# Dealing out two side generators more tightly: HGRN's steps earlier, some gate steps last

## The chip, the cores and the metric

The kernel runs on one core of a Trainium2 chip. The metric is the device time of one execution in microseconds (us); before the change the median of three runs was 3617.13 us (3607.03 to 3620.99). A profiled execution took 3613.31 us.

## The reference

Two networks run one after the other on 512 tokens of width 1024. The change is in the first block, which mixes three branches:

```python
xn = rmsnorm(x, norm1_w[l])
p = xn @ w_in[l]
z, xbc, dt_raw, p_rwkv, p_hgrn, p_gate = jnp.split(p, in_splits, axis=-1)
y_ssm = ssd_branch(z, xbc, dt_raw, ...) @ w_branch_ssm[l]
y_rwkv = rwkv7_branch(p_rwkv, ...) @ w_branch_rwkv[l]
y_hgrn = hgrn2_branch(p_hgrn, ...) @ w_branch_hgrn[l]
gates = jax.nn.sigmoid(p_gate).reshape(b, L, N_BRANCH, D_MODEL)
mixed = gates[:, :, 0] * y_ssm + gates[:, :, 1] * y_rwkv + gates[:, :, 2] * y_hgrn
x = x + mixed @ w_out[l]
```

The RWKV branch is a delta-rule recurrence in two directions for 8 heads of 64; the HGRN branch is a gated linear recurrence in two directions for 4 heads of 128; the gates are 24 blocks of 128 columns of the projection. The second block (attention, a neighbourhood attention, an mLSTM and a differential attention, twice) is not touched.

## The kernel before

Every projection is held in float16 halves: a block of 128 x 128 weights takes three matmuls (high x high, high x low, low x high) of 512 columns each. Weights come in units of 8 blocks (512 KB). `_emit_unit` loads a unit with a DMA on SP's queue, ScalarE writes the high half (L1070) and VectorE the low half (L1071). There are two buffer pairs for the foreground (`whi`, `wlo`) and two for the background (`bhi`, `blo`). Units are prefetched in the order of two written lists, FOREGROUND and BACKGROUND; `take` checks that the code uses them in just that order, and a unit's pair comes free when its last matmul has read it.

The first phase (`first`, pool `f_rwkv`) runs RWKV in four stages of two heads. A stage j is `rwkv_mid` (products with the decays, matrices G, a loop of 31 rows in which VectorE solves triangular blocks at L464 and L467, with DMAs before and behind it to turn the data round) and then `rwkv_scan` (8 chunks, each a chain TensorE to VectorE and back; its first VectorE instruction is L526), and at the end `rwkv_out`. Inside the scan of stage j, at chunk 2, `rwkv_in` makes the inputs of stage j + 1: it takes three weight units and uses the PSUM bank `acc`; at chunk 4 come their decays.

Two Python generators are dealt out between those steps by `beside(g, h)`. It adds g to what is due of the gates and h to what is due of HGRN, and advances each by its whole steps. A gate step is one weight block, three matmuls into the bank `bg1`, with 8 steps in a gate block and 192 in all; the gates use the foreground's list. HGRN has 15 steps a head and 60 in all: 5 of projections, 7 levels, 2 states, 1 output; its weights are of the background's list and its projections use `bg0`. `beside` is called 7 times in `rwkv_mid` (each fourth row) and 8 times in `rwkv_scan`. What is left behind the last stage is traced by `beside(1000, 1000)`. Then the pool closes and SSD begins (`ssd`, its first instruction is `dsk` at L617), with the three up-projections as background behind it.

The order in which this is traced is a priority, not the order on the engines: a scheduling pass goes through the program with a model of times and gives each engine, whenever it is free, the earliest traced instruction that is ready. The order that it finds is then fixed, and each engine executes its own in order. So a traced step may be drawn ahead of its place where its buffers, banks and weights allow it. A tile of a new pool waits until the tiles that lay there before are done.

Of the kernel before, what the change touches and what calls it, by code (L numbers as in the profile page):

```python
# [226 lines left out]
def run(gen):  # L227

    try:
        while True:  # L230
            next(gen)
    except StopIteration as e:
        return e.value

class First:
# [39 lines left out]
    def rwkv(self, yd, beside):  # L275


        nc, v = self.nc, self.nc.vector
        mid = self.mid
        it = self.block_iter("w1", 0, 14)  # L280
        self.mu2 = self.t(mid, [128, 14], "mu2")
        v.tensor_tensor(out=self.mu2, in0=self.col("mu0", 0, 14), in1=self.col("mu1", 0, 14), op=ALU.add)
        v.tensor_scalar(out=self.mu2, in0=self.mu2, scalar1=-1.0, scalar2=1.0, op0=ALU.mult, op1=ALU.add)
        self.hb = self.t(mid, [128, 12], "hb1")
        v.tensor_scalar(out=self.hb, in0=self.col("wa0", 0, 12), scalar1=0.5, scalar2=None, op0=ALU.mult)
        self.ka1 = self.t(mid, [128, 4], "ka1")
        v.tensor_scalar(out=self.ka1, in0=self.col("ka", 0, 4), scalar1=-1.0, scalar2=1.0, op0=ALU.mult, op1=ALU.add)
        self.lwh, self.lwl = (self.t(mid, [128, 3, T], n, F16) for n in ("lwh", "lwl"))
        for n in range(3):
            lw = self.w()  # L290
            nc.sync.dma_start(out=lw, in_=self.io["lora"][:, n])
            self.split(self.lwh[:, n], self.lwl[:, n], lw, WS)
        lx, gx = (tuple(self.t(mid, [128, T], n + p, F16) for p in "hl") for n in ("lx", "gx"))
        c = self.w()
        run(self.shifted(it, 12, c))
        nc.scalar.activation(out=c[0:64], in_=c[0:64], func=AF.Tanh)
        self.split(*lx, c)
        c = self.w()
        run(self.shifted(it, 13, c))
        nc.scalar.activation(out=c, in_=c, func=AF.Tanh, scale=0.5)  # L300
        v.tensor_scalar(out=c, in0=c, scalar1=0.5, scalar2=0.5, op0=ALU.mult, op1=ALU.add)
        self.split(*gx, c)
        self.hsel = self.load(mid, "hsel", [128, 2])
        self.hexp = self.load(mid, "hexp", [2, 128])
        self.hones = self.load(mid, "hones", [128, 128])
        self.rwm = self.load(mid, "rwm", [128, 2, 128])
        self.reset = self.t(mid, [128, T + 64], "reset")
        v.memset(self.reset, 1.0)
        v.memset(self.reset[:, 0::64], 0.0)  # L309
        run(self.rwkv_in(0, it, lx))  # L310
        self.rwkv_decays(0, lx)
        for j in range(4):
            self.rwkv_mid(j, beside)
            scan = self.rwkv_scan(j)
            for c in range(8):
                if c == 2 and j < 3:
                    run(self.rwkv_in(j + 1, it, lx))
                if c == 4 and j < 3:
                    self.rwkv_decays(j + 1, lx)
                next(scan)  # L320
                beside(2.5, 1)
            run(scan)
            self.rwkv_out(j, gx, yd)

# [72 lines left out]
    def rwkv_mid(self, j, beside):  # L397
# [61 lines left out]
        for i in range(31):  # L459
            ts, nt = slice(i + 1, 32), 31 - i  # L460
            rs = [(c, (i - 2 * c) // 4 + 1) for c in range(2) if i >= 2 * c]
            for c, n in rs:
                t = tx[c][:, 0:n * nt].rearrange("p (a b) -> p a b", b=nt)
                v.tensor_tensor(out=t, in0=X[c][:, 0:n, i:i + 1].to_broadcast([128, n, nt]), in1=M[:, i:i + 1, ts].to_broadcast([128, n, nt]), op=ALU.mult)  # L464
            for c, n in rs:
                t = tx[c][:, 0:n * nt].rearrange("p (a b) -> p a b", b=nt)
                v.tensor_tensor(out=X[c][:, 0:n, ts], in0=X[c][:, 0:n, ts], in1=t, op=ALU.subtract)  # L467
            if i % 4 == 3:
                beside(3.5, 0.9)
        pd2 = self.t(self.dram, [2, 32, 8, 2, 2, 32], "pd2")  # L470
        for q in range(2):
            for c in range(2):
# [491 lines left out]
class Net(First):  # L964
# [1160 lines left out]


FOREGROUND = [
# [35 lines left out]
```

## Time and profile before

| | |
|---|---|
| median of three runs | 3617.13 us |
| profiled execution | 3613.31 us |
| its span, first to last instruction | 3611.6 us |
| instructions | 60781 |
| TensorE busy | 3338.2 us (92%) |
| VectorE busy | 2760.1 us (76%) |
| ScalarE busy | 1608.3 us (45%) |
| GpSimd busy | 752.6 us (21%) |
| granted TensorE clock, mean | 0.976 |

Busy time counts from an instruction's start to its end. Matmuls overlap, so a busy TensorE is not one at its peak: the distance between two starts tells how many go in a microsecond. Times in the rows count from the span's start. The first phase lies in the first fifth of the span.

### The profile page before, as it was taken

To read this page: it belongs to the slowest core of one execution; us is meant where nothing else is said; L and a number is where in the kernel's file an instruction comes from. 1 tells how busy PE (TensorE), PEld (TensorE's weight loads), DVE (VectorE), ACT (ScalarE), POOL (GpSimd) and SP (SyncE) were. 2 spreads that over 40 slices of the span, in tenths; PEclk is the share of its full clock that TensorE was granted. 3 is DMA by queue.
4 is the path that set the end of the run, shared out by engine and by line. 5 is a ranking of instruction groups with operands and counts; after the bars stand their busy time and mean duration, and the time that the engine had idled before them with its cause. 6 is when DMAs were issued, how large, how long until landed. Compare 5 with 4: busy or idle time off the path is not lost. (4 is left out here: it accounts for less than half of the span.)

```text
span 3611.6 us, 60781 instructions
## 1 busy us (share of the span) xinstructions
PE 3338.2 (92%) x23758; PEld 2033.9 (56%) x23758; DVE 2760.1 (76%) x5599; ACT 1608.3 (45%) x3009; POOL 752.6 (21%) x782
## 2 busy tenths in 40 slices
PE   7899999899899999999989999999999989999998
PEld 3565566555455577556545545568655545545567
DVE  6877777587777798788767677788788767777788
ACT  4232333255344344464556543344364455534443
POOL 2222223223332211201221132211201120132211
PEclk9999999899899999999999999999999999999999
DMA  4312213233242234323223353335322323363333
GB/s 141 82 57 59 75 49 91 72 126 114 88 164 94 94 106 146 106 63 96 93 82 109 116 159 96 96 112 159 111 65 80 94 90 100 112 185 110 94 100 94
DMA packets 151156, 368.16 MB, mean 102 GB/s; under 512 B 44098, under 2 KB 47428, under 8 KB 150868
## 3 DMA queue, kind: packets, MB, share of 16 engines
q1 hardware_dynamic: 117492, 336.03, 30.0%
q0 software_dynamic: 7680, 23.00, 1.9%
q10 hardware_dynamic: 25696, 5.25, 0.8%
q8 instruction: 186, 3.05, 0.4%
q14 instruction: 102, 0.84, 0.1%
HBM read 322.72 MB, written 40.04 MB: 100 GB/s over the span
## 5 line engine op out<-in xcount | busy, mean ns | idle before, releaser
L1181 PE MATMUL acc<-xh,whi 128*128 128x512 f16 x1224 | 469.5, 384 | 28.3 <-DVE g L1706 7.5
L1183 PE MATMUL acc<-xh,wlo 128*128 128x512 f16 x1224 | 469.0, 383 | 23.7 <-DVE wlo L1071 23.6
L1182 PE MATMUL acc<-xl,whi 128*128 128x512 f16 x1224 | 468.9, 383 | 0.0
L1070 ACT ACTIVATE whi<-wst 128x1024 f16<-128x1024 f32 x264 | 275.3, 1049 | 310.3 <-PE acc L1182 147.1
L1071 DVE SCALAR_TENSOR_TENSOR wlo<-wst,whi 128x1024 f16<-128x1024 f32 x264 | 353.9, 1341 | 15.9 <-ACT whi L1070 14.3
L1183 PEld LDWEIGHTS <-wlo 128*128 128x128 f16 x1824 | 179.6, 98 | 257.3 <-DVE wlo L1071 51.4
L1182 PEld LDWEIGHTS <-whi 128*128 128x128 f16 x1824 | 179.9, 99 | 226.6 <-issue 41.9
L1181 PEld LDWEIGHTS <-whi 128*128 128x128 f16 x1824 | 180.6, 99 | 210.4 <-issue 12.4
L1183 PE MATMUL bg<-xh,blo 128*128 128x512 f16 x596 | 230.9, 387 | 3.4 <-DVE reset L309 3.2
L1181 PE MATMUL bg<-xh,bhi 128*128 128x512 f16 x596 | 230.9, 387 | 0.4 <-DVE hk L810 0.4
L1182 PE MATMUL bg<-xl,bhi 128*128 128x512 f16 x596 | 230.6, 387 | 0.0
L1440 POOL TENSOR_TENSOR w<-w,w 128x512 f32<-128x512 f32 x66 | 117.5, 1780 | 448.4 <-DVE w L1440 282.1
L1216 PE MATMUL acc<-whi,xh 128*128 128x128 f16 x1152 | 195.1, 219 | 3.1 <-DVE xp L1758 1.3
L1218 PE MATMUL acc<-whi,xl 128*128 128x128 f16 x1152 | 195.0, 219 | 0.0
L1217 PE MATMUL acc<-wlo,xh 128*128 128x128 f16 x1152 | 195.0, 219 | 0.0
L1070 ACT ACTIVATE bhi<-bst 128x1024 f16<-128x1024 f32 (+1 forms) x132 | 121.7, 934 | 129.4 <-PE bg L1182 89.7
L1071 DVE SCALAR_TENSOR_TENSOR blo<-bst,bhi 128x1024 f16<-128x1024 f32 (+1 forms) x132 | 160.8, 1223 | 13.7 <-ACT bhi L1070 12.1
L1183 PE MATMUL bg<-xh,wlo 128*128 128x512 f16 x408 | 157.3, 386 | 9.1 <-DVE wlo L1071 9.1
L1181 PE MATMUL bg<-xh,whi 128*128 128x512 f16 x408 | 157.4, 386 | 3.0 <-ACT whi L1070 1.8
L1182 PEld LDWEIGHTS <-bhi 128*128 128x128 f16 x980 | 97.6, 100 | 109.0 <-issue 20.1
L1183 PEld LDWEIGHTS <-blo 128*128 128x128 f16 x980 | 97.5, 100 | 106.9 <-issue 6.8
L1181 PEld LDWEIGHTS <-bhi 128*128 128x128 f16 x980 | 97.9, 100 | 105.4 <-issue 9.8
(666 smaller groups left out, 9256.9 us busy)
## 6 DMA issues: line engine op xcount, KB each, us to landing
wst<-win SPq DMA_DIRECT2D x92, 512.0 KB, 3.6
bst<-win SPq DMA_DIRECT2D x64, 512.0 KB, 3.7
wst<-wff SPq DMA_DIRECT2D x60, 512.0 KB, 3.5
wst<-w SPq DMA_DIRECT2D x58, 512.0 KB, 3.6
gd<-bw SPq DMA_DIRECT2D x88, 256.0 KB, 2.2
ug<-gd SPq DMA_DIRECT2D x88, 256.0 KB, 2.7
wst<-wf SPq DMA_DIRECT2D x30, 512.0 KB, 3.5
bst<-w SPq DMA_DIRECT2D x20, 512.0 KB, 3.6
```

Source lines behind the costliest of these rows:

```text
L1070: nc.scalar.activation(out=hi[:, h], in_=st[:, h], func=AF.Copy, scale=WS)
L1071: nc.vector.scalar_tensor_tensor(out=lo[:, h], in0=st[:, h], scalar=WS, in1=hi[:, h], op0=ALU.mult, op1=ALU.subtract)
L1181: mm(ps, lhsT=wh, rhs=h[:, k, :], start=(k == 0), stop=False)
L1182: mm(ps, lhsT=wh, rhs=l[:, k, :], start=False, stop=False)
L1183: mm(ps, lhsT=wl, rhs=h[:, k, :], start=False, stop=(k == nk - 1))
L1216: mm(o, lhsT=xh, rhs=wh, start=(k == 0), stop=False)
L1217: mm(o, lhsT=xh, rhs=wl, start=False, stop=False)
L1218: mm(o, lhsT=xl, rhs=wh, start=False, stop=(k == 7))
L1440: tt = lambda eng, o, x, y, op=ALU.add: eng.tensor_tensor(out=o, in0=x, in1=y, op=op)
```

## The change

In the scan each chunk deals out 2 gate steps and 1.25 HGRN steps, where it was 2.5 and 1; in the mid part each fourth row deals out 3 and 1.1, where it was 3.5 and 0.9. The foreground's weight list follows the new order of use: between RWKV's second and third group of units stand four gate units instead of six, and behind the last group eleven instead of nine.

```diff
                 next(scan)
-                beside(2.5, 1)
+                beside(2, 1.25)
             run(scan)
...
             if i % 4 == 3:
-                beside(3.5, 0.9)
+                beside(3, 1.1)
...
 FOREGROUND = [
-    ("w1", 0, 5), ("w1", 14, 18), ("w1", 5, 8), ("w1", 18, 24), ("w1", 8, 11), ("w1", 24, 29),
-    ("w1", 11, 14), ("w1", 29, 58), ("wo1", 0, 8), ("wf1", 0, 2), ("wf1s", 0, 1), ("wf1", 2, 6),
+    ("w1", 0, 5), ("w1", 14, 18), ("w1", 5, 8), ("w1", 18, 22), ("w1", 8, 11), ("w1", 22, 27),
+    ("w1", 11, 14), ("w1", 27, 58), ("wo1", 0, 8), ("wf1", 0, 2), ("wf1s", 0, 1), ("wf1", 2, 6),
```

Units 0 to 13 of `w1` are RWKV's (the first two for the low-rank inputs, then three a stage), 14 to 37 the gates', 38 to 57 SSD's.

## Rows read from the trace of the kernel before

**Rows 1.** Busy time by stretch: RWKV's four stages, and behind them.

```profile
core 0: us, PE busy (x) PEld busy (x) DVE busy (x) ACT busy (x) POOL busy (x), PEclk, DMA share, GB/s
97.90:235.90 138.00, 126.74 (x1046) 84.26 (x1045) 107.72 (x276) 42.17 (x91) 36.18 (x36) 0.98 0.24 66
235.90:398.30 162.40, 150.40 (x1133) 97.42 (x1132) 122.62 (x308) 49.83 (x103) 45.80 (x43) 0.94 0.22 64
398.30:544.30 146.00, 138.33 (x1094) 90.68 (x1093) 113.25 (x297) 47.49 (x93) 40.60 (x36) 0.98 0.23 66
544.30:677.50 133.20, 124.49 (x1037) 85.82 (x1037) 95.19 (x271) 43.80 (x92) 42.09 (x29) 0.97 0.25 75
677.50:712.00 34.50, 20.33 (x165) 13.57 (x164) 15.96 (x61) 4.05 (x15) 7.32 (x10) 0.61 0.34 117
```

**Rows 2.** Timeline, VectorE, L526 in stage 1's scan: start us, us, engine, line.

```profile
308.23 0.42 DVE L526 TENSOR_SCALAR w<-O 64x256 f32<-64x256 f32 x1
...
321.47 0.42 DVE L526 TENSOR_SCALAR w<-O 64x256 f32<-64x256 f32 x1 [0.48 <-PE O L524]
...
347.88 0.41 DVE L526 TENSOR_SCALAR w<-O 64x256 f32<-64x256 f32 x1
...
367.31 0.41 DVE L526 TENSOR_SCALAR w<-O 64x256 f32<-64x256 f32 x1
```

**Rows 3.** Groups, TensorE, 128 to 174 us: xcount | busy us, mean ns | idle before.

```profile
L1183 PE MATMUL acc<-xh,wlo 128*128 128x512 f16 x24 | 10.1, 422 | 1.9 <-DVE wlo L1071 1.9
```

**Rows 4.** Groups, TensorE, 300 to 345 us.

```profile
L1183 PE MATMUL acc<-xh,wlo 128*128 128x512 f16 x24 | 9.4, 391 | 0.0
```

**Rows 5.** Timeline, ScalarE, splits of weights in stage 1's scan.

```profile
327.73 1.06 ACT L1070 ACTIVATE whi<-wst 128x1024 f16<-128x1024 f32 x1 [1.89 <-PE acc L1182]
...
343.43 1.06 ACT L1070 ACTIVATE whi<-wst 128x1024 f16<-128x1024 f32 x1 [7.81 <-PE acc L1182]
```

**Rows 6.** Timeline, VectorE, L526 in stage 3's scan: first, seventh and eighth.

```profile
616.19 0.42 DVE L526 TENSOR_SCALAR w<-O 64x256 f32<-64x256 f32 x1
...
666.43 0.42 DVE L526 TENSOR_SCALAR w<-O 64x256 f32<-64x256 f32 x1 [1.86 <-PE O L524]
...
672.61 0.42 DVE L526 TENSOR_SCALAR w<-O 64x256 f32<-64x256 f32 x1 [1.77 <-PE O L524]
```

**Rows 7.** Timeline, all engines, the end of the phase and SSD's start.

```profile
686.42 1.27 POOL L586 TENSOR_TENSOR w<-w,bon 128x512 f32<-128x512 f32 x1 [3.37 <-DVE w L585]
...
694.50 0.69 DVE L917 TENSOR_TENSOR hw<-hw,hg 128x512 f32<-128x512 f32 x1
...
696.46 0.17 DVE L617 TENSOR_SCALAR dsk<-cols 128x8 f32<-128x8 f32 x1 [1.27 <-PE H L1547]
...
701.43 0.42 ACT L1231 ACTIVATE wdh<-wdt 128x256 f16<-128x256 f32 x1 [4.17 <-DMA wdt<-wdt]
```

**Rows 8.** Timeline, TensorE, two matmuls of a row.

```profile
155.36 0.38 PE L1183 MATMUL acc<-xh,wlo 128*128 128x512 f16 x1
155.57 0.38 PE L1181 MATMUL acc<-xh,whi 128*128 128x512 f16 x1
```

**Rows 9.** Groups, TensorE, 25 to 700 us, HGRN's largest.

```profile
L1181 PE MATMUL bg<-xh,bhi 128*128 128x512 f16 x95 | 38.4, 404 | 0.4 <-DVE hk L810 0.4
...
L1216 PE MATMUL bg<-bhi,xh 128*128 128x128 f16 x256 | 49.8, 235 | 13.2 <-DVE hi L816 9.9 <-DVE hk L810 3.3
...
L852 PE MATMUL H<-hw,hw 128*128 128x128 f32 x160 | 25.2, 291 | 9.6 <-DVE tx L464 6.0 <-DVE hs L832 2.4 <-DVE hw L847 1.3
```

**Rows 10.** Groups, VectorE, 25 to 700 us: weight splits, HGRN's level operations.

```profile
L1071 DVE SCALAR_TENSOR_TENSOR wlo<-wst,whi 128x1024 f16<-128x1024 f32 x38 | 53.2, 1399 | 3.0 <-ACT whi L1070 2.0 <-PE bg L1183 0.9
...
L867 DVE TENSOR_TENSOR hp<-hp 128x512 f32<-128x512 f32 x28 | 24.7, 882 | 0.4
...
L846 DVE TENSOR_TENSOR hw<-hq,hp 128x512 f32<-128x512 f32 x28 | 22.4, 799 | 0.1
```

**Rows 11.** One line's instructions, L867: ns min/median/max, first and last start.

```profile
L867 DVE TENSOR_TENSOR hp<-hp x28: 673/692/1751, 136.0 to 658.9; 128x512 f32<-128x512 f32 x28
```

## The prediction

> **What bounds the kernel now.** I read the page's line of 40 slices first: in the first phase TensorE is at 7 to 9 tenths and VectorE at 7 to 8, so neither is simply full. Then the busy time by stretch, cut at the start of each RWKV stage [rows 1]. The reader is to see three things in it. The four stages have nearly the same work and take 138.0, 162.4, 146.0 and 133.2 us (the last has no inputs of a next stage to make). In all four TensorE is busy for 92 to 95% and VectorE for 71 to 78%. And behind the last stage lies a gap, 677.5 to 712 us, in which TensorE is busy for 20.3 of 34.5 us at a granted clock of 0.61, which is between its two levels of 1.2 and 2.4 GHz, and VectorE for 16.0 us.
>
> Then I read the steps of the RWKV scan in the timeline of VectorE, by their first instruction there, L526. In stage 1 most follow each other in about 7 us, but from 321.47 to 367.31 us two take 45.84 us together; the two before them took 13.24 [rows 2]. What lies there? By the groups of TensorE, the three weight units of RWKV's next inputs (24 matmuls of each of three lines, into the bank acc) run at 300 to 345 us, inside that scan [rows 4]; in stage 0 the same work ran at 128 to 174 us, inside the mid part, ahead of the scan, which starts at 172 [rows 3]. ScalarE's splits of those units in stage 1 both wait for the last matmul of the unit before (releaser PE acc L1182), 15.7 us apart [rows 5]: the other pair of weight buffers is held by a gate unit. So the order of the weight list, not any engine, puts this work into the scan: in stage 0 four gate units stand between RWKV's third-last and next units, in stage 1 six.
>
> Last, the end. HGRN's last head closes after RWKV: RWKV's last read of its own pool is GpSimd's L586, 686.42 + 1.27 = 687.69 us; HGRN's last product ends at 695.19, and SSD's first instruction, dsk, starts at 696.46, waiting for the transposes of it [rows 7]. The pool of the first phase must be empty before SSD's tiles are written.
>
> **The change part by part.** Per stage there are 7 calls in the mid part and 8 in the scan. HGRN gets 7 x 1.1 + 8 x 1.25 = 17.7 steps where it got 7 x 0.9 + 8 = 14.3; gates get 7 x 3 + 8 x 2 = 37 where they got 44.5. HGRN has 60 steps, so three stages take 53.1 of them (42.9 before) and the last 6.9 fall into the mid part of stage 3: its scan has none. Of 192 gate steps 148 are dealt out and 44 stay for the end, where 14 did, and none of HGRN's where 2.8 did. No instruction and no DMA is added or taken away; the weight and gate DMAs on SP's queue move with their steps.
>
> *HGRN's tail.* It no longer ends the phase; RWKV's output does. 696.46 - 687.69: -8.8 us, if RWKV ends where it did.
>
> *Scan of stage 3.* Seven intervals take 672.61 - 616.19 = 56.4 us with HGRN beside them; the last, where HGRN has little left, takes 6.18 [rows 6]. Floor 7 x 6.18 = 43.3, so between 0 and -13.1. Gates still run between the steps, so I take the middle: -7.
>
> *Weight order.* Between units 7 and 8 stand four gate units instead of six, so RWKV's inputs of stage 2 can be made in the mid part, as in stage 0; between 10 and 11 there are still five, but all of them begin two units earlier. Stage 1 is 162.4 - 138.0 = 24.4 us longer than stage 0, stage 2 8.0. Bounds 0 and -32.4: half of each, as the work must still run somewhere: -12 and -4.
>
> *HGRN's closer steps in stages 0 to 2.* 10.2 steps more, 22.5 gate steps fewer. On TensorE matmuls of 512 columns start 0.21 to 0.22 us apart [rows 8], so a gate step, three of them, is 0.645 us. HGRN's largest groups: 95 matmuls beside two groups like it, 3 x 95 x 0.215 = 61 us; a block of three interleaved groups, 49.8; L852 25.2 [rows 9]; together 136 us over 60 steps, 2.3 each. Net 10.2 x 2.3 - 22.5 x 0.645 = +9 us. On VectorE the four level operations take 22.4 to 24.7 us (first and last of four groups), 93 us, 1.55 a step; a gate unit's split is 1.40 per 8 steps [rows 10]. Net 10.2 x 1.55 - 2.8 x 1.40 = +12 us. If both are hidden in idle time, 0; if neither, +21. TensorE's share in these stages is the nearest to full, so I take its +9.
>
> A closer look at one of these costs: L867 takes 692 ns as a median and up to 1751 [rows 11]. The Trainium skill (GPSIMD Engine Reference, section Specifications) says that GpSimd shares its SBUF interfaces with VectorE and that instructions with two SBUF inputs contend; HGRN's level operations are such, and HGRN's own GpSimd work comes closer together. If every one of the 10.2 x 7/15 = 4.8 levels moved ahead had all four operations stretched from 0.80 to 1.75 us, the sum would rise by another 4.8 x 4 x 0.95 = 18 us; the median says that most are not, and the mean used above holds those that are.
>
> *The tail of gates.* 44 steps x 0.645 = 28 us of TensorE. They have nothing to wait for but their weights and one bank, and lie beside RWKV's last output and SSD's start: 34.5 us in which TensorE's busy time is 20.3 us at clock 0.61, so 12.4 us at full clock, 22 us open. The rest goes into pauses of the last scan, so I cost them at nothing. If that cover is gone, each step costs 0.645 us, at most 28 us, as SSD's matmuls are traced behind them and their weights stand in the same list. What is late next is then SSD's wdt, which lands 4.7 us after dsk in any case [rows 7].
>
> Sum: -8.8 - 7 - 12 - 4 + 9 = -23 us (the gain has room: the four stages and the gap hold 11.3 + 12.0 + 7.7 + 8.7 + 22 = 62 us in which TensorE isn't used). The profiled execution took 3613.3 us (span 3611.6), 3.8 below the median of three, 3617.1. 3613.3 - 23 = 3590; by the median 3594. I give 3594.
>
> **The rivals.**
> *A, nothing much* (3613): the scheduling pass already pulls HGRN and gates ahead of where they are traced, and the unit order only moves the crowding by a stage; then only HGRN's tail and part of the last scan go, and the closer steps give it back: -8.8 - 7 + 12 = -4, by the median 3613. For it: TensorE is busy for over 92% in each stage. Against it: 22 us of the gap have no filler at all.
>
> *B, slower* (3643). One mechanism: a gate unit that is half read when RWKV takes its three units holds one of the two buffer pairs, and each unit must pass through the other, split after matmul. At the third scan step 5, 2 and 6 of 8 blocks were read in stages 0, 1 and 2; now 1, 6 and 3. Price, from stage 1: 45.84 - 13.24 = 32.6 us for the stage where it bites [rows 2]. If it moves into stage 0, and stage 1 keeps its share because HGRN's projections hold VectorE there: +32.6 + 9 - 8.8 - 7 = +26, 3639; by the median 3643. It decides from the point where RWKV's units start after the scan has begun; against it, stage 0's list is the same four units as before, and there they were through before the scan.
>
> *C, much faster* (3571): both bounds at once, -8.8 - 13.1 - 24.4 = -46, if the denser HGRN goes wholly into idle time: 3613.3 - 46 = 3567, by the median 3571. For it: VectorE's 22 to 29% idle. Against: all stages would be as short as the best one.
>
> **How the numbers follow.** The forecast (3580 to 3606 on its own) gets 0.46, A 0.27, B 0.14, C 0.13. Two or three runs of this kernel differ by up to 14 us; under 0.5%, 18 us, no change can be told. Faster by more (below 3599): 0.37 of the forecast's 0.46 and C's 0.13, 0.50. Slower by more (above 3635): B's upper part and a little beyond, 0.13. Within: 0.37. The range reaches from C to the lower part of B: 3570 to 3630.
>
> **What would show it.** Right: the L526 intervals in the scan of stage 1 all under 15 us, and RWKV's three units there ahead of the scan; stage 3's intervals near 7 us; dsk waiting for RWKV's L586 or its neighbours and not for HGRN; gate matmuls between 660 and 700 us, and the granted clock there near 1. Wrong: an interval of 20 us or more in any scan (B), stages 0 to 2 each longer by 7 us or more, or gate matmuls that hold SSD's first ones.

## The result, and the profile after

The changed kernel takes 3667.1 us (median of 4 runs, 3665.4 to 3676.4), the kernel before 3612.3 beside it (4 runs, 3607.0 to 3621.0): a ratio of 1.0155, with a 95% interval of 1.0125 to 1.0184. It is slower by 55 us, where 3594 and a range of 3570 to 3630 had been forecast.

The profiled execution after took 3668.59 us, with a span of 3666.8 (+55.2). The same view as in [rows 1], cut at the same instructions (each stage's first G, L428; the last sum of RWKV, L563; the end of the gap behind it):

```profile
95.80:241.60 145.80, 128.90 (x1038) 85.84 (x1036) 109.55 (x281) 43.10 (x92) 34.58 (x35) 0.93 0.19 53
241.60:423.50 181.90, 162.68 (x1329) 107.86 (x1328) 129.77 (x346) 53.19 (x107) 49.57 (x45) 0.94 0.23 65
423.50:601.20 177.70, 151.31 (x1173) 97.30 (x1173) 137.28 (x322) 51.38 (x105) 49.88 (x42) 0.95 0.21 57
601.20:735.70 134.50, 117.44 (x794) 74.18 (x793) 76.84 (x216) 36.25 (x82) 27.16 (x20) 0.86 0.24 71
735.70:762.00 26.30, 11.76 (x126) 6.13 (x125) 12.96 (x48) 3.74 (x7) 7.48 (x10) 0.61 0.46 150
```

The stages take 145.8, 181.9, 177.7 and 134.5 us where they took 138.0, 162.4, 146.0 and 133.2. No engine is nearer to full for it: in stage 2 TensorE is busy for 85% (95% before), VectorE for 77%. So this view says where the time is lost, not on what.

Each stage divides further at three instructions: the middle part (first G to the first scan step L526), in it the loop of 31 triangular rows (first L464 to last L467), the scan (to the last sum L563), and the gap from there to the next stage's first G, or behind stage 3 to SSD's dsk. Starts taken from the timelines of the two kernels, differences in us:

| | rows of the loop | rest of the middle | scan | gap behind |
|---|---|---|---|---|
| before, stages 0 to 3 | 35.2, 22.7, 25.3, 28.6 | 39.0, 49.6, 45.6, 43.3 | 63.9, 89.6, 74.7, 61.3 | 0, 0.4, 0.4, 18.9 |
| after, stages 0 to 3 | 39.5, 48.4, 41.5, 28.2 | 43.0, 50.3, 46.9, 52.5 | 63.4, 72.1, 74.2, 53.8 | -0.2, 11.1, 15.1, 11.3 |
| sum of the change | +45.8 | +15.2 | -26.0 | +17.6 |

With 2.1 us less before the first G, dsk comes 50.6 us later (696.46 to 747.04), and what follows takes 4.7 more. The scans gained 26.0 us, where 23 had been forecast of them; the row loops, the rest of the middles and the gaps together lost 78.6, three times as much.

What is in the loop? The busy time of each engine in the loops of stages 0 to 2, of the kernel before and then of the one after (columns as in [rows 1]; the stretches of stage 0 end 1.3 and 1.7 us before the loop does):

```profile
115.90:149.80 33.90, 25.99 (x157) 14.75 (x155) 32.83 (x137) 7.88 (x11) 8.90 (x5) 0.95 0.19 55
260.80:283.60 22.80, 18.95 (x184) 14.25 (x182) 22.37 (x127) 6.25 (x9) 3.36 (x2) 0.87 0.29 95
423.30:448.40 25.10, 18.56 (x169) 12.64 (x168) 25.08 (x127) 6.39 (x10) 5.62 (x3) 0.93 0.29 94
```

```profile
115.70:153.50 37.80, 26.55 (x127) 15.20 (x125) 36.28 (x143) 7.13 (x10) 10.93 (x7) 0.82 0.17 48
266.20:314.60 48.40, 39.22 (x285) 23.72 (x283) 48.03 (x158) 13.39 (x20) 13.09 (x9) 0.96 0.19 63
449.80:491.20 41.40, 29.62 (x161) 15.77 (x162) 40.84 (x144) 10.73 (x18) 15.61 (x12) 0.84 0.24 76
```

Here, and not in the stage as a whole, one engine is full: in stage 1 VectorE is busy for 22.37 of 22.80 us before and 48.03 of 48.40 after. Its groups in the loop of stage 1, first before, then after (count, busy us, mean ns):

```profile
L464 DVE TENSOR_TENSOR tx<-X,M 128x60 f32<-128x60 f32 (+34 forms) x60 | 11.8, 237 | 0.4 <-DMA M<-pd 0.4
L467 DVE TENSOR_TENSOR X<-X,tx 128x60 f32<-128x60 f32 (+34 forms) x60 | 10.9, 222 | 0.0
```

```profile
L464 DVE TENSOR_TENSOR tx<-X,M 128x60 f32<-128x60 f32 (+34 forms) x60 | 16.3, 306 | 0.0
L467 DVE TENSOR_TENSOR X<-X,tx 128x60 f32<-128x60 f32 (+34 forms) x60 | 11.8, 237 | 0.0
L867 DVE TENSOR_TENSOR hp<-hp 128x512 f32<-128x512 f32 x6 | 5.2, 863 | 0.0
L846 DVE TENSOR_TENSOR hw<-hq,hp 128x512 f32<-128x512 f32 x7 | 4.8, 686 | 0.0
L847 DVE TENSOR_TENSOR hw<-hk,hr 128x512 f32<-128x512 f32 x6 | 4.1, 683 | 0.0
L866 DVE TENSOR_TENSOR hr<-hr,hp 128x512 f32<-128x512 f32 x6 | 4.1, 682 | 0.0
```

All seven levels of an HGRN head begin in this loop; before there was none. Counted by L846, the loops of stages 0 to 3 held 3, 0, 0, 0 levels and hold 4, 7, 3, 0; HGRN's VectorE time (of the operations that start there) was 11.6, 2.3, 4.1, 4.8 us and is 14.4, 24.7, 14.8, 3.3. The timeline of VectorE shows how they come in (start, us):

```profile
291.64 0.34 DVE L464 TENSOR_TENSOR tx<-X,M 128x60 f32<-128x60 f32 x2
291.90 0.34 DVE L467 TENSOR_TENSOR X<-X,tx 128x60 f32<-128x60 f32 x2
292.16 0.68 DVE L846 TENSOR_TENSOR hw<-hq,hp 128x512 f32<-128x512 f32 x1
292.76 0.68 DVE L847 TENSOR_TENSOR hw<-hk,hr 128x512 f32<-128x512 f32 x1
293.37 0.22 DVE L464 TENSOR_TENSOR tx<-X,M 128x66 f32<-128x66 f32 x1
293.50 0.68 DVE L866 TENSOR_TENSOR hr<-hr,hp 128x512 f32<-128x512 f32 x1
```

A line of L464 or L467 with x2 is a pair of operations, one on each of the tiles X0 and X1. A row of the loop, a pair of products and a pair of differences, takes 0.5 us (291.64 to 291.90 to 292.16); each level operation between two rows puts the next 0.6 us back.

In the scans, L526 answers to [rows 2] and [rows 6]: stage 1 first (first, third, fourth and last of 8), then stage 3 (first, second, last):

```profile
340.22 0.42 DVE L526 TENSOR_SCALAR w<-O 64x256 f32<-64x256 f32 x1
...
358.00 0.42 DVE L526 TENSOR_SCALAR w<-O 64x256 f32<-64x256 f32 x1 [2.68 <-PE O L524]
368.80 0.42 DVE L526 TENSOR_SCALAR w<-O 64x256 f32<-64x256 f32 x1
...
404.00 0.41 DVE L526 TENSOR_SCALAR w<-O 64x256 f32<-64x256 f32 x1
```

```profile
681.89 0.42 DVE L526 TENSOR_SCALAR w<-O 64x256 f32<-64x256 f32 x1
692.37 0.42 DVE L526 TENSOR_SCALAR w<-O 64x256 f32<-64x256 f32 x1 [1.23 <-PE O L524]
...
731.04 0.42 DVE L526 TENSOR_SCALAR w<-O 64x256 f32<-64x256 f32 x1 [0.28 <-PE O L524]
```

In stage 1 the longest interval is 10.8 us; the 45.84 us for two are gone. RWKV's three weight units, inside the scan in [rows 4], now run ahead of most of it: the matmuls of the last one end at 344.7, 4.5 us after the first L526. In stage 3 seven intervals take 49.2 us (56.4 before). The end of the phase, which answers to [rows 7]:

```profile
745.75 1.26 POOL L586 TENSOR_TENSOR w<-w,bon 128x512 f32<-128x512 f32 x1 [3.55 <-DVE w L585]
747.04 0.17 DVE L617 TENSOR_SCALAR dsk<-cols 128x8 f32<-128x8 f32 x1 [1.37 <-POOL w L586]
752.68 0.42 ACT L1231 ACTIVATE wdh<-wdt 128x256 f16<-128x256 f32 x1 [3.68 <-DMA wdt<-wdt]
```

dsk waits for RWKV's L586 and no longer for HGRN, as forecast.

The gaps between stages are new. The one behind stage 2, on VectorE:

```profile
580.88 1.43 DVE L846 TENSOR_TENSOR hw<-hq,hp 128x512 f32<-128x512 f32 x1
582.23 0.68 DVE L847 TENSOR_TENSOR hw<-hk,hr 128x512 f32<-128x512 f32 x1
...
587.79 1.74 DVE L847 TENSOR_TENSOR hw<-hk,hr 128x512 f32<-128x512 f32 x1
589.45 0.21 DVE L568 BATCH_NORM_STATS2 st<-M 128x6 f32<-128x64 f32 x1
...
592.00 1.54 DVE L412 TENSOR_TENSOR kr<-fr,eps 128x512 f32<-128x512 f32 x1
...
598.45 2.81 DVE L577 TENSOR_SCALAR M<-M,mv,rs 128x64 f32<-128x64 f32 x8 [1.54 <-POOL rs L1238]
601.17 0.68 DVE L428 TENSOR_TENSOR G<-S,rwm 128x512 f32<-128x512 f32 x1
```

HGRN's levels stand ahead of the products (L412) from which the next G is made, and the first G stands behind the whole norm of the stage's output (L568 to L577).

### The profile page after: what moved, and what is told of

It reads as the page before. It is cut to its first block, busy times and chain, and to the rows that moved or that the text cites. A ratio compares the mean times of both kernels' runs of the same rounds, so it can differ in the third digit from the quotient of the medians.

```text
span 3666.8 us, 60829 instructions
## 1 busy us (share of the span) xinstructions
PE 3352.6 (91%) x23758; PEld 2034.5 (55%) x23758; DVE 2774.7 (76%) x5599; ACT 1609.7 (44%) x3009; POOL 747.6 (20%) x782
## 5 line engine op out<-in xcount | busy, mean ns | idle before, releaser
L1183 PE MATMUL acc<-xh,wlo 128*128 128x512 f16 x1224 | 472.0, 386 | 28.1 <-DVE wlo L1071 28.0
L1071 DVE SCALAR_TENSOR_TENSOR blo<-bst,bhi 128x1024 f16<-128x1024 f32 (+1 forms) x132 | 160.6, 1220 | 10.1 <-ACT bhi L1070 8.6
L1182 PE MATMUL bg<-xl,whi 128*128 128x512 f16 x408 | 159.5, 391 | 0.0
L1182 PEld LDWEIGHTS <-bhi 128*128 128x128 f16 x980 | 97.4, 99 | 104.6 <-issue 16.3
```

What stands on the lines that cost most here:

```text
L1071: nc.vector.scalar_tensor_tensor(out=lo[:, h], in0=st[:, h], scalar=WS, in1=hi[:, h], op0=ALU.mult, op1=ALU.subtract)
L1182: mm(ps, lhsT=wh, rhs=l[:, k, :], start=False, stop=False)
L1183: mm(ps, lhsT=wl, rhs=h[:, k, :], start=False, stop=(k == nk - 1))
```

## The experiments

Two theories were put against each other. *Place* (P in the expectations): RWKV's row loop is bound by VectorE, so what counts is which HGRN steps fall into it. A head has 15 steps, 5 of projections (TensorE) and then 7 levels (VectorE); at 14.3 steps a stage the projections stay beside the rows, at 17.7 everything slides forward by 2.7 steps a stage, and the levels come to lie there. *Rate* (R): HGRN's faster pace costs its work wherever it lies. E1 and E2 also test a third, *gates* (G): the gates' part of the change costs the time. Each loop, middle (its loop included) and scan below is the sum over the four stages; the gaps are the three between stages. These columns and dsk are read from one profiled execution each; that of E8 took 17 us more than its median, the others are within 7 us of theirs.

| run | HGRN steps per call, scan / middle | gates | loops | middles | scans | gaps | dsk at | ratio to before, 95% |
|---|---|---|---|---|---|---|---|---|
| before | 1 / 0.9 | old | 111.8 | 289.3 | 289.5 | 0.8 | 696.5 | |
| after | 1.25 / 1.1 | new | 157.6 | 350.3 | 263.5 | 26.0 | 747.0 | 1.0125 to 1.0184 |
| E1 | 1.25 / 1.1 | old | 160.2 | 357.9 | 283.3 | 28.6 | 774.6 | 1.0185 to 1.0227 |
| E2 | 1 / 0.9 | new | 119.4 | 299.4 | 274.7 | 2.5 | 706.8 | 1.0010 to 1.0040 |
| E4 | 1.25 / 0.714 | old | 102.6 | 300.3 | 291.6 | 0.2 | 704.9 | 1.0006 to 1.0036 |
| E5 | 1 / 0.9, 7 ahead | old | 162.7 | 360.7 | 252.2 | 21.1 | 771.6 | 1.0178 to 1.0213 |
| E6 | 1 / 1 | new | 147.5 | 336.2 | 290.0 | 4.2 | 737.7 | 1.0118 to 1.0162 |
| E7 | 1.22, 6 calls / 1.1 | new | 143.0 | 343.8 | 273.4 | -0.2 | 724.6 | 1.0059 to 1.0128 |
| E8 | as after, rows first | new | 144.3 | 334.2 | 291.9 | 26.0 | 758.7 | 1.0110 to 1.0166 |
| E9 | as before, rows first | old | 115.9 | 291.3 | 289.1 | 4.1 | 702.8 | 1.0014 to 1.0036 |
| E10 | 1.25 / 0.714 | new | 113.6 | 290.8 | 277.6 | 25.2 | 701.5 | 1.0035 to 1.0065 |
| E11 | 1.1 / 0.88 | new | 117.3 | 320.1 | 282.6 | -2.2 | 712.4 | 1.0073 to 1.0100 |
| E12 | 1.1 / 0.88 | old | 116.9 | 310.3 | 289.1 | 0.2 | 712.1 | 1.0015 to 1.0035 |
| E13 | as E10, output traced later | new | 112.2 | 292.9 | 279.5 | 13.8 | 693.4 | 1.0023 to 1.0046 |

By the time alone neither theory wins: P's range held in E5 and E10, R's in E4, E7, E8, E9 and E12, both in E2, neither in E1, E6 and E11 (E13 tests something else). What decides about place are the two pairs in which the pace is the same and the place is not: E5 against before, and E6 against E10.

**E1 and E2, the two halves of the change.** E1 is the kernel before with HGRN's numbers alone, E2 the one after with HGRN's numbers put back.

```diff
 E1, against before
-beside(2.5, 1)
+beside(2.5, 1.25)
-beside(3.5, 0.9)
+beside(3.5, 1.1)
```

```diff
 E2, against after
-beside(2, 1.25)
+beside(2, 1)
-beside(3, 1.1)
+beside(3, 0.9)
```

> HGRN's share of the change alone: 1.25 and 1.1 steps, gates dealt out at 2.5 and 3.5 and listed as before. Theory P (place): 17.7 steps a stage are not a head's 15, so HGRN's levels slide into the row loops of stages 1 and 2, where VectorE has no idle time; expected 3650 to 3680 us, with the row loops of stages 1 and 2 over 35 us each. Theory R (rate): the mere density of HGRN's work in the first three stages costs; also 3650 to 3680, but spread over mid parts and scans alike. Theory G (gates): the fewer gate units between RWKV's and the longer tail cost; then this kernel is at 3600 to 3620.

> The gates' share of the change alone: 2 and 3 gate steps with the changed weight list, HGRN dealt out at 1 and 0.9 as before. Theories P and R: no loss of the changed kernel's kind, 3590 to 3625 us, row loops of 22 to 34 us as before. Theory G: 3640 to 3670.

E1 takes 3688.2 us, E2 3622.3, before 3611.7: the loss is HGRN's share, and G is out. E1 lies above the 3650 to 3680 that P and R both gave. The halves do not add up: +77 and +11 us, but +55 together. Beside HGRN's new pace the new gates save 21 us (E1 to after), beside its old pace they cost 11. They shorten the scans in both cases (19.8 and 14.8 us); only beside the old pace do they lengthen the middles (+10.1) and HGRN's tail (+15.2). In E1 the loops are 37.7, 53.1, 42.2 and 27.2 us, with the same 4, 7, 3 and 0 levels as after. The gates' half does in stage 1 what was forecast of it: middle and scan 137.5 us there (161.9 before), with the L526 intervals 7 to 11 us. It loses that again in stage 0's middle (+12) and in HGRN's tail, the gap behind stage 3, which grows from 18.9 to 34.1.

**E4, the projections left in the middle part.** 5 steps there and 10 in the scan, a whole head a stage, with the old gates.

```diff
 E4, against before
-beside(2.5, 1)
+beside(2.5, 1.25)
-beside(3.5, 0.9)
+beside(3.5, 5 / 7 + 1e-6)
```

> Gates as before; HGRN gets 5 steps in each mid part (5/7 a call) and 10 in each scan (1.25 a chunk), a whole head in each stage, so that the five projections are dealt out in the row loop and levels, states and output in the scan. Theory P: row loops of 22 to 34 us in all four stages in spite of the scan's 1.25, and 3585 to 3615 us. Theory R: the scan is as dense as in the changed kernel and each stage gets 15 steps instead of 14.3, so 3620 to 3640.

3622.9 us: P's loops came true (22.6 to 28.7 us), but the time lies in R's range. The loops are shorter than in the kernel before (102.6), and two levels, not three, fall into stage 0's; the rest of the middles grows by 20 us, and the time does not follow the loops alone.

**E5, the same pace at another place.** HGRN's numbers as before, but seven steps are traced ahead of RWKV, so that the levels lie where the projections did.

```diff
 E5, against before
+        beside(0, 7)
         run(self.rwkv_in(0, it, lx))
```

> The kernel before with one line more: 7 HGRN steps are traced ahead of stage 0. Rates and weight lists are as before, so each stage gets 14.3 steps, but now the levels of a head begin in the mid part. Theory P: the row loops of most stages grow by 10 to 25 us, 3640 to 3690 us. Theory R: no stage is denser, HGRN ends sooner, 3590 to 3615.

3684.7 us, 73 more than before, at the old pace and with the old gates. The loops, which lengthen from stage to stage as the slide goes the other way:

```profile
161.00:189.30 28.30, 23.05 (x107) 14.01 (x106) 26.47 (x140) 6.71 (x16) 6.36 (x9) 0.82 0.22 67
302.20:339.60 37.40, 29.82 (x167) 15.69 (x167) 34.60 (x143) 10.86 (x20) 13.09 (x11) 0.86 0.25 79
460.10:503.90 43.80, 32.34 (x171) 16.15 (x172) 40.80 (x144) 12.51 (x20) 16.61 (x12) 0.86 0.26 77
623.00:676.30 53.30, 36.64 (x199) 20.10 (x200) 48.60 (x155) 12.05 (x20) 17.36 (x14) 0.87 0.21 64
```

They hold 0, 2, 3 and 6 levels. Some 30 us of E5 are the seven steps themselves, as the first G starts at 127.6 instead of 97.9. The other 43 us come at the old pace: pace is not needed for the loss, place is enough.

**E6 and E10, a head a stage, placed in two ways.** Both have the gates of the change and 15 steps a stage; E6 puts 7 of them beside the rows, E10 5. E10 differs from the changed kernel in one number.

```diff
 E6, against after
-beside(2, 1.25)
+beside(2, 1)
-beside(3, 1.1)
+beside(3, 1)
```

```diff
 E10, against after
-beside(3, 1.1)
+beside(3, 5 / 7 + 1e-6)
```

> The changed kernel's gates (2 and 3, changed weight list), with HGRN dealt out at exactly 1 and 1: 15 steps, one head, in each stage. Theory P (place): no level slides into a row loop, so loops of 22 to 40 us, the scan of stage 1 near 70 us as with the gates alone, and HGRN ends with RWKV, so that the 34 us between RWKV's last sum and SSD fall to 12 to 20: 3595 to 3612 us. Theory R (rate): 15 instead of 14.3 steps a stage add a fifth of the changed kernel's loss, 3625 to 3640.

> The changed kernel with one number undone: HGRN's share in the mid part 5/7 a call instead of 1.1, the scan's 1.25 and all of the gates as changed. A stage gets 5 + 10 = 15 steps, the five projections in the mid part. Theory P (place): row loops by 22.5 + 1.2 x HGRN's VectorE time in them, so 22 to 32 us in all four stages, and 3600 to 3630 us. Theory R (rate): the scan keeps the changed kernel's density, 3640 to 3665.

E6 takes 3665.9 us, E10 3628.3, a pair 38 us apart with the same pace. I had expected 3595 to 3612 of E6, and missed, for I had counted steps a stage and not what lies in the loop: of 7 steps 5 are projections, and two or more levels fall into every loop (4, 3, 2, 3; loops 147.5 us). E10's loops hold 3, 1, 0 and 0, nearly as before the change, and its time lies in P's range. The loops of stages 0 and 1, first in E6, then in E10:

```profile
114.40:153.80 39.40, 29.12 (x135) 16.86 (x134) 37.89 (x145) 7.10 (x10) 12.72 (x8) 0.78 0.19 57
292.10:328.40 36.30, 28.26 (x232) 20.15 (x229) 36.14 (x142) 7.81 (x11) 11.65 (x6) 0.91 0.28 87
```

```profile
115.50:150.60 35.10, 26.45 (x158) 15.15 (x156) 33.51 (x140) 9.04 (x12) 9.45 (x5) 0.95 0.23 73
265.10:289.70 24.60, 18.36 (x163) 13.88 (x161) 23.06 (x127) 6.76 (x11) 3.79 (x3) 0.86 0.29 101
```

Undoing one number of the change brings back 39 of 55 us (loops 44.0 shorter than after, middles 59.5).

**E7, the changed kernel capped to a head a stage.** The middle part as changed; in the scan 7.3 steps over the first six chunks.

```diff
 E7, against after
-beside(2, 1.25)
+beside(2, 7.3 / 6 if c < 6 else 0)
```

> The changed kernel, but HGRN's scan share is dealt out in the first six chunks only (7.3 / 6 = 1.217 each, then 0), so that a stage gets 7.7 + 7.3 = 15 steps: nearly as dense as the changed kernel in 13 of 15 calls, without the slide. Theory P: row loops of 25 to 40 us, 3600 to 3630 us. Theory R: the density stays in the mid part and in most of the scan, 3640 to 3665.

3643.7 us: in R's range, not in P's. The loops are of the lengths that P gave (32.7 to 39.4 us), but that is still 31 us more than before: with 7.7 steps beside the rows, levels stay in them (4, 3, 2, 2), and P's time was too good for the same reason as in E6. The gaps between stages are gone, which fits that no step of HGRN is dealt out beside the last two chunks.

**E8 and E9, the rows first.** The two loops over the rows' operations are traced with a higher priority, in the changed kernel (E8) and in the one before (E9).

```diff
 E8 against after, E9 against before
+            with self.tc.high_priority():
                 for c, n in rs:
 ...
```

> The changed kernel with the two operations of the row loop traced at high priority, so that the scheduling pass puts them ahead of whatever else is ready on VectorE; amounts and places of the trace as in the changed kernel. Theory P, in the form that HGRN's levels stand ahead of the rows on VectorE: row loops of 22 to 30 us in all stages, and of the 46 us that the loops of stages 0 to 2 grew, at least half comes back, 3615 to 3645 us. Theory R: the work is only moved behind the loop, 3655 to 3675.

> The kernel before with the row loop's two operations at high priority. Theory P: only stage 0's loop was long (35 us) and falls to 22 to 28; 3600 to 3615 us, no more than 10 us gained. Theory R: the same as before, 3605 to 3620.

3659.4 and 3619.5 us: both numbers of P missed, and both of R held. If the levels took only turns that a row could have had, priority would have cured it. It did so in part, in stage 1, whose loop fell from 48.4 to 33.0 us and from 7 levels to 3; the others are still 39.4, 41.8 and 30.1 us. As R said, the work moved behind the loop: the scans are 28 us longer than in the changed kernel. One reading of the rest is that a row isn't ready when the last one has just been issued, and the pass gives VectorE whatever is ready in that moment: a level operation of 0.68 us between pairs of 0.2 to 0.35. Then priority does not guard a chain of short operations that each wait for the one before. This fits E8, but no run shows it by itself.

**E11 and E12, a head a stage at nearly the old pace.**

```diff
 E11, against after
-beside(2, 1.25)
+beside(2, 1.1)
-beside(3, 1.1)
+beside(3, 0.88)
```

```diff
 E12, against before
-beside(2.5, 1)
+beside(2.5, 1.1)
-beside(3.5, 0.9)
+beside(3.5, 0.88)
```

> The changed kernel's gates, HGRN at 0.88 in the mid part and 1.1 in the scan: 6.2 + 8.8 = 15.0 steps a stage, so nearly nothing of HGRN is left for the end, where the gates alone left 34 us between RWKV's last sum and SSD. Theory P: the mid part gets hardly more than with the gates alone (6.3 steps), so row loops of 23 to 40 us with no drift, the end's 34 us fall to 12 to 20, 3598 to 3612 us. Theory R: 0.7 steps a stage more, a fifth of the changed kernel's loss, 3625 to 3640.

> The kernel before with HGRN at 0.88 and 1.1, gates untouched: again 15.0 steps a stage. Theory P: row loops as before, SSD's start some 7 us sooner, 3600 to 3612 us. Theory R: 3618 to 3630.

3641.0 and 3620.4 us, both slower than P gave; E12 lies in R's range, E11 1 us above it. The loops are near the old ones (117.3 and 116.9), as P says; but the rest of the middles is 25 and 16 us longer than before (202.8 and 193.4 against 177.5). Place in the row loop is thus not the whole cost of a new dealing.

The first G only divides this cost: what is a gap in E10 is rest of the middle in E11. Taken together (middles less loops, and gaps), the two are 178 to 183 us before, in E2 and in E9, and 193 to 202 in all seven kernels that deal out 15 steps a stage (E4, E6, E7 and E10 to E13). HGRN's VectorE time in these stretches is 38 to 45 us in the first three and 54 to 63 in the seven. So a head a stage costs 15 to 24 us there; that HGRN's work makes it is likely, but no run shows it by itself.

**E13, the output traced behind the next G.** What is left of E10's loss lies in its gaps. There the first G of stage 2 starts at 389.37 us, though the products for it are done by 382.7; on TensorE and VectorE, in E10:

```profile
381.53 1.16 PE L425 MATMUL S<-kr,bk 64*128 64x128 f32 x14
```

```profile
388.25 1.20 DVE L577 TENSOR_SCALAR M<-M,mv,rs 128x64 f32<-128x64 f32 x5
389.37 0.68 DVE L428 TENSOR_TENSOR G<-S,rwm 128x512 f32<-128x512 f32 x1
```

G stands behind the norm in VectorE's fixed order. In E13 the output of a stage is traced later:

```diff
 E13, against E10
             run(scan)
-            self.rwkv_out(j, gx, yd)
+        self.rwkv_out(3, gx, yd, self.bon)
 ... (in rwkv_mid, behind the DMAs from G)
+        if j:
+            self.rwkv_out(j - 1, gx, yd, last)
```

> E10 with one thing moved: RWKV's output of a stage (the sum L563, the norm, the transposes) is traced behind the G matrices of the next stage and their DMA, where it was traced ahead of them. In E10 the next stage's first G stands in VectorE's order behind the norm: its products had ended at 382.7 us and it started at 389.37, and the gaps between a stage's last sum and the next G were 2.7, 9.7 and 12.8 us, 25.2 together (0.8 in the kernel before). If the order alone makes these gaps (call it the theory of the output's place): they fall to some 0 to 2 us each, about 20 us go, and the run takes 3600 to 3615 us, so that what is left of the change's gain would show against 3610 of the kernel before. If VectorE's and TensorE's work of that stretch makes them, or the norm only moves into the way of the triangular rows behind G: 3622 to 3635, with the gaps gone and the middle parts longer by as much.

3621.7 us beside 3610.4: between the two expectations, and by the intervals not told apart from E10. The gaps fall from 25.2 to 13.8 us, the rest of the middles grows by 3.5, and dsk comes 8.1 earlier, at 693.4, so the order made about half of the gaps. G still starts at 387.62, now behind the first of HGRN's two last products (L919); what makes the other half stays open. E13 ends its first phase 3.1 us before the kernel before does, and is still slower: gate work is left behind dsk (see the tail of gates below).

## Why the prediction was wrong, step by step

*HGRN's closer steps in stages 0 to 2* is the step that failed. It was costed at +9 us, with bounds of 0 and +21, as an amount of work against the idle time of a whole stage. It took TensorE's share, as the nearest to full; in the row loop of stage 1 TensorE is busy for 18.95 of 22.80 us and VectorE for 22.37. VectorE's 22 to 29% idle is a mean over a stage [rows 1]; in that loop it has 2%. Measured: +45.8 us in the loops, +15.2 in the rest of the middles, and +25 in the gaps between stages; HGRN's half of the change alone (E1) costs 77 us. The amount was about right: four stages of VectorE hold 453.4 us of its work by the first four rows of after, 438.8 before [rows 1], +14.6 where +12 was forecast. What was missed is where 17.7 steps a stage would put a head of 15.

The price of the place can be read from all loops at once: over the 56 row loops of the 14 kernels, a straight line through length against HGRN's VectorE time inside gives 22.3 us + 1.20 us for each us (correlation 0.945). So 14.4 + 24.7 + 14.8 + 3.3 - 22.8 = 34.4 us more of HGRN make about 41 of the 45.8. One reason that it is more than 1 is that RWKV's own rows are stretched too, from 22.7 to 28.1 us in stage 1. The stretched ones lie beside GpSimd's work; VectorE, then GpSimd, in the changed kernel:

```profile
289.49 1.41 DVE L464 TENSOR_TENSOR tx<-X,M 128x70 f32<-128x70 f32 x2
290.82 0.34 DVE L467 TENSOR_TENSOR X<-X,tx 128x70 f32<-128x70 f32 x2
...
295.69 1.42 DVE L464 TENSOR_TENSOR tx<-X,M 128x60 f32<-128x60 f32 x2
```

```profile
289.37 1.32 POOL L855 TENSOR_TENSOR hs<-hs,hw 128x512 f32<-128x512 f32 x1 [1.23 <-DVE hw L854]
...
295.60 1.31 POOL L855 TENSOR_TENSOR hs<-hs,hw 128x512 f32<-128x512 f32 x1 [4.92 <-DVE hw L854]
```

A pair of row operations takes 1.41 us instead of 0.35 while L855, which adds an HGRN level to its sum, runs on GpSimd. Of the 480 row operations 28 take over 0.5 us in the changed kernel and 13 before, all beside a GpSimd operation: HGRN's own in 17 cases (3 before), the gates' (L1322) or the low half of a background weight unit, which GpSimd makes for some of them (L1067), in 11 (10 before). Against 0.2 us for each, that is some 33 us of waiting where it was 17, so about a third of the loops' growth. The prediction looked for this in HGRN's own operations and priced it at 18 us at most; it falls on the rows too, about 1 us a time. The Trainium skill (GPSIMD Engine Reference, section Specifications) says that the two engines share their SBUF interfaces and that VectorE's instructions with two SBUF inputs contend; these rows agree with it.

*Weight order* was right in its mechanism: the scan of stage 1 is 17.5 us shorter, and in E2 middle and scan together 24.4, which is the bound; the forecast was 12. Half had been kept back because the work must still run somewhere, and in E2 stage 0's middle is 12 us longer; whether that is the same work, no run shows. In stage 2 (forecast -4) the scan gained 0.5: nothing.

*Scan of stage 3*: 61.3 to 53.8, -7.5, forecast -7. *HGRN's tail*: the gap 18.9 to 11.3, -7.6, forecast -8.8. Both as said.

*The tail of gates* was costed at nothing, and in the changed kernel that came true, but in another place: no gate matmul stands behind dsk there, and only 9 of the tail's 132 start behind RWKV's last sum. The rest were drawn ahead into stage 3. So the gap was not filled, though the prediction had counted on it: TensorE is busy for 11.76 of its 26.30 us, again at a granted clock of 0.61. Where gate matmuls are left behind dsk, the tail costs something. From dsk to the end the kernel before takes 2915.1 us. E6, E7, E10, E11 and E13, with 40 to 62 gate matmuls behind dsk, take 4.9 to 10.1 us more; the other eight, with none, differ by -4.9 to +4.7. With one execution of each this is no more than a few us; the bound was 28.

*Rivals.* A (nothing much, 3613) and C (3571) did not come true. B, the slower one, named another mechanism (a half-read gate unit) and 3643; the longest interval in any of the four scans is about 11 us, and the scans are shorter in sum. So B's sign came true and its reason did not. The prediction's own sign of failure did show: stages 0 to 2 longer by 7.8, 19.5 and 31.7 us.

What stays open: what makes the 15 to 24 us more between a stage's last sum and the next scan, outside the row loop, in every kernel with a head a stage (the rest of the middles in E11 and E12, half of E10's gaps). No version tried beats the kernel before; the best (E2, E4, E9, E12) are 0.2% slower.

## What to carry to other kernels

Side work that is dealt out evenly still has a phase: compare its steps per stage with the steps per unit of its own period, and write down which of its steps fall beside which part of the main chain, stage by stage. Look for the stretch in which one engine is full, however short, and cost there with that engine's own time, not with the idle share of the whole stage. Keep the steps of the full engine out of that stretch by where they are dealt out; a higher priority for the chain alone did not do it here.

## What the runs showed of the hardware

Not expected in its place: a small operation of VectorE with two inputs in SBUF, 0.2 us by itself, took 1.3 us beside a GpSimd operation of 1.3 us on 128 x 512. Over the 14 kernels, 261 of the 6720 row operations took more than 0.5 us. Each of them lies beside a GpSimd operation and ends 0.02 to 0.10 us behind the end of one; of the 5994 with no GpSimd operation beside them, none took more than 0.24 us. So these 261 waited until the GpSimd operation ended, however small they were, and a small one pays far more in proportion than the 128 x 512 ones of [rows 11] (0.69 to 1.75).
